# Linear attention: decays of the gates worked out ahead of the values' projection, two logarithms queued behind two exponentials

## The chip, the cores and the metric

The kernel runs on one core of one Trainium2 chip. The metric is device time in microseconds (us), the median of the runs shown. The engines are TensorE (PE, with its weight loads as PEld), VectorE (DVE), ScalarE (ACT), GpSimd (POOL) and SyncE (SP, which only issues transfers here).

## The reference

One layer of a generator. Two token mixers, a gated linear attention (GLA, 4 heads) and a gated delta rule (GDN, 8 heads), read the same normed input of 1024 latent and 256 context tokens; their outputs are gated, merged and projected, a feed-forward network follows, and a norm. The change is within GLA:

```python
def gla_prepare(q, k, v, lr_f, lr_b, lr_w, lr_bias):        # heads of 128 (q, k) and 256 (v)
    gates = tuple(log_sigmoid(lr @ lr_w[d] + lr_bias[d]) / 16 for d, lr in ((0, lr_f), (1, lr_b)))

def step(S, inp):                                            # gla_scan, chunk by chunk, in both directions
    qc, kc, vc, gc = inp
    G = cumsum(gc, axis=-2)
    decay = exp(where(incl[:, :, None], G[..., :, None, :] - G[..., None, :, :], -inf))
    A = einsum('bhid,bhjd,bhijd->bhij', qc, kc, decay)
    o = einsum('bhij,bhjv->bhiv', A, vc) + einsum('bhid,bhdv->bhiv', qc * exp(G), S)
    S = exp(G_end)[..., None] * S + einsum('bhjd,bhjv->bhdv', kc * exp(G_end - G), vc)
```

## The kernel before, in words

Three phases follow one another. **Phase 1** (to about 797 us) holds the input norm and, for each of the four GLA heads in turn, `gla_head`, and then six projections with convolution for GDN (`gdn_conv`, six behind each head by `CONVS`). **Phase 2** is the GDN scan with the merges, **phase 3** the output projection and the feed-forward network.

Products with large weights run as three matmuls of split operands (`mm3`, L174 to L176). The weights come by `wcols`: `wsplit` loads a tile on SP's queue (`wraw`, tag "wr", 2 buffers) and splits it into `whi` on ACT (L156) and `wlo` on DVE (L157), tags "wh" and "wl", 4 buffers each. The values of a head need four such tiles, other projections of a head two.

A head works in this order: queries (L443), keys (L450), values (`v`, five pairs of chunks through the three banks "pj", copied out on DVE at L458), in head 0 the low-rank input of the gates and its loads (`gla_lowrank`), then the **decays**. Of these, L471 makes the gates' logits (three matmuls for each direction, banks "ch", of which there are three), L472 and L474 take the absolute value and the minimum with zero, L477 the exponential, L479 the logarithm, L483 and L490 sum along the chunks, L498 takes the decay of a chunk. `decayed_keys` (L502 to L520) multiplies the keys by a decay (`e`, L514), transposes them on PE (L517) and copies them out (`kt`, L519); L528 and L538 multiply them with `v` into the states `S` (L529, L539). The attention over seven levels follows (L544 to L610), then the six convolutions: projection, copies out of the banks on ACT (L788 to L792), taps on DVE (L797, L800), a tanh (L802) and a product (L803). `mod_rows`, called behind the keys, adds up a row of the modulation on DVE (L1092).

Each engine works off its own list in order. The lists are laid out at compile time by a planner that takes, of what its own clock holds to be ready, what stands earliest in the program; `high_priority` moves an instruction forward, and `issue_after` ties the instructions of a block on one engine behind a given one. So work that stands later, such as a convolution's projection, fills in where a head waits. `q`, `k`, `v`, `G` and `S` have one buffer each: a head can write them only when the head before has read them for the last time.

Of the kernel before, what the change touches and what calls it, by code (L numbers as in the profile page):

```python
# [8 lines left out]
F32 = mybir.dt.float32  # L9
# [3 lines left out]
AF = mybir.ActivationFunctionType  # L13
# [4 lines left out]
P = 128  # L18
D = 1024
KT = D // P  # L20
# [3 lines left out]
NCH = TT // P  # L24
# [7 lines left out]
C_GQ, C_GK, C_GV, C_GZ, C_LR, _, C_DQ, C_DK, C_DV, C_DZ, C_AB, C_G1, C_G2 = (int(o) for o in OFF[:13])  # L32
# [46 lines left out]
class Layer:  # L79
# [354 lines left out]
    def gla_head(self, h):  # L434
        nc, I, g1, g2 = self.nc, self.I, self.g1, self.g2
# [3 lines left out]
        w = self.wcols(I['w_in'], C_GQ + h * P) if h else self.first  # L439
        for t0, n in spans[:2]:  # L440
            ps = self.pj(P, 512)
# [4 lines left out]
        w = self.wcols(I['w_in'], C_GK + h * P)  # L446
        for t0, n in spans:
            ps = self.pj(P, 512)[:, 0:n]
            self.proj(ps, w, t0, n)
            nc.scalar.activation(k[:, t0:t0 + n], ps, AF.Copy)  # L450
        yield 1
        v = g1.tile([P, NCH, 256], F32, name="v")
        w = self.wcols(I['w_in'], C_GV + h * 256, 256)
        for c0 in range(0, NCH, 2):
            ps = self.pj(P, 2, 256)
            for c in (c0, c0 + 1):
                self.mm3(ps[:, c - c0, :], [self.xparts(kk, c * P, P) + w[kk] for kk in range(KT)])
            nc.vector.tensor_copy(v[:, c0:c0 + 2, :], ps)  # L458
        yield 2
        if h == 0:  # L460
            self.gla_lowrank()

# [3 lines left out]
        ts = [s.rearrange("p c n -> p (c n)")[:, 0:TT] for s in S]  # L466
        zs = []
        for d, t in enumerate(ts):
            for t0, n in spans:
                ps = self.ch(P, 512)[:, 0:n]  # L470
# [3 lines left out]
                    nc.vector.tensor_scalar(G[:, 0, t0:t0 + n], ps, 0.0, None, ALU.min)  # L474
                zs.append(ps)
        for t in ts:
            nc.scalar.activation(t, t, AF.Exp, scale=-1.0)  # L477
        for t in ts:
            nc.scalar.activation(t, t, AF.Ln, bias=1.0)  # L479
        chunks = [(c * P, P) for c in range(8)] + [(T, TC)]  # L480
        for c0, n in chunks:
            g = G[:, 0, c0:c0 + n]
# [14 lines left out]
        for d in range(2):  # L497
            nc.scalar.activation(dec[d], end[d], AF.Exp, scale=1.0 / 16)  # L498

        def decayed_keys(d, c0, nch):  # L500

            lo, n = c0 * P, nch * P  # L502
            e = g2.tile([P, 4, P], F32, tag="e", name="e", bufs=4)
            ef = e.rearrange("p c i -> p (c i)")[:, 0:n]
            if d == 1:
                nc.scalar.activation(ef, G[:, 1, lo:lo + n], AF.Exp, scale=1.0 / 16)
            else:
                if lo < T:
                    nc.vector.tensor_tensor(e[:, 0:nch], end[0][:, c0:c0 + nch].unsqueeze(2).broadcast_to([P, nch, P]),
                                            Gf[:, c0:c0 + nch], ALU.subtract)  # L510
                else:
                    nc.vector.tensor_scalar(ef, G[:, 0, lo:lo + n], G[:, 0, TT - 1:TT], -1.0, ALU.subtract, ALU.mult)
                nc.scalar.activation(ef, ef, AF.Exp, scale=1.0 / 16)
            nc.vector.tensor_tensor(ef, ef, k[:, lo:lo + n], ALU.mult)  # L514
            ps = self.wk(P, 4, P)
            for c in range(nch):
                nc.tensor.transpose(ps[:, c, :], e[:, c, :], self.ident)  # L517
            kt = g2.tile([P, 4, P], F32, tag="kt", name="kt", bufs=2)
            nc.scalar.activation(kt[:, 0:nch], ps[:, 0:nch], AF.Copy)  # L519
            return kt  # L520


        for d in range(2):
            first = 0 if d == 0 else 7
            kt = decayed_keys(d, 8, 2)
            ps = self.ch(P, 512)[:, 0:256]
            for c in range(2):
                nc.tensor.matmul(ps, kt[:, c, :], v[:, 8 + c, :], start=(c == 0), stop=(c == 1))  # L528
            nc.scalar.activation(S[d][:, first, :], ps, AF.Copy)  # L529
            self.dump(f"gla_s{h}_{d}", S[d][:, first, :])  # L530
            for half in ((0, 1) if d == 0 else (1, 0)):
                cs = (range(0, 4), range(4, 7)) if d == 0 else (range(1, 4), range(4, 8))
                cs = cs[half]
                kt = decayed_keys(d, cs[0], len(cs))
                for c in (cs if d == 0 else reversed(cs)):
                    nxt = c + 1 if d == 0 else c - 1
                    ps = self.ch(P, 512)[:, 0:256]
                    nc.tensor.matmul(ps, kt[:, c - cs[0], :], v[:, c, :], start=True, stop=True)  # L538
                    nc.vector.scalar_tensor_tensor(S[d][:, nxt, :], S[d][:, c, :], dec[d][:, c:c + 1], ps, ALU.mult, ALU.add)  # L539
# [4 lines left out]
        for half in range(2):  # L544
            c0, lo = 4 * half, 512 * half
# [5 lines left out]
            ps = self.wk(P, 4, P)  # L551
# [4 lines left out]
            for li, s in enumerate(LEVELS):  # L556
# [19 lines left out]
                ps = self.wk(P, 4, P)  # L576
# [12 lines left out]
            for c in range(c0, c0 + 4):  # L589
                cs = slice((c - c0) * P, (c - c0) * P + P)  # L590
                ps = self.ch(P, 512)[:, 0:256]
# [12 lines left out]
            for j in range(2):  # L604
                ps = self.wk(P, 4, P)
# [823 lines left out]
```

## Time and profile before

| | |
|---|---|
| runs | 2364.49, 2360.04, 2384.71 us; median 2364.49 |
| the profiled execution | 2363.35 us, its span 2361.6 us |
| busy share of the span | PE 96%, PEld 80%, DVE 73%, ACT 49%, POOL 4% |
| mean granted TensorE clock | 0.985 of full speed |

The profiled execution spends 1.75 us outside its span. A busy share is a mean over stages: DVE with 73% is nearly full in some stretches of phase 1 and nearly empty in others. The granted clock has two levels, 1.2 and 2.4 GHz, shown as 0.50 and 1.00.

### The profile page before, as it was taken

What the parts mean: (1) busy time and instruction counts of PE and PEld (TensorE: products, weight loads), DVE (VectorE), ACT (ScalarE), POOL (GpSimd) and SP (SyncE); (2) the same over time, 40 slices, a digit from 0 to 9 for tenths busy, and PEclk for the clock granted to TensorE, in tenths of its full rate; (3) what the DMA queues carried; (4) which work ended last, traced back from release to release, by engine and by line L of the source; (5) the groups of instructions that cost most, each with busy time, mean ns of one, the idle gap of its engine ahead of it and who ended that gap; (6) DMA issues with size and microseconds to landing.
All of it is one profiled execution on the core that took longest, in us unless ns stands there. A gap on an engine that the chain in (4) does not pass through costs nothing. (4 is left out here: it accounts for less than half of the span.)

```text
span 2361.6 us, 37155 instructions
## 1 busy us (share of the span) xinstructions
PE 2273.9 (96%) x13604; PEld 1885.6 (80%) x13604; DVE 1713.0 (73%) x4087; ACT 1167.6 (49%) x2803; POOL 96.7 (4%) x190
## 2 busy tenths in 40 slices
PE   7999999999999899999999999989999999999998
PEld 4988888888888777877787787768778888888886
DVE  6579669669669675988888788565687777783454
ACT  6265355355355556678678776643433333341221
POOL 0000000000000100000000000000000000000000
PEclk9999999999999999999999998999999999999999
DMA  8212402401501542323323332233132222264221
GB/s 287 68 38 72 148 18 64 161 19 60 165 18 59 171 116 81 114 74 100 109 81 96 101 110 71 90 133 131 54 112 94 85 76 90 77 205 138 88 77 58
DMA packets 208166, 230.82 MB, mean 98 GB/s; under 512 B 14835, under 2 KB 170811, under 8 KB 207983
## 3 DMA queue, kind: packets, MB, share of 16 engines
q1 hardware_dynamic: 189040, 171.18, 24.5%
q0 software_dynamic: 14688, 50.92, 5.9%
q10 hardware_dynamic: 4255, 6.35, 0.9%
q8 instruction: 107, 1.75, 0.3%
q14 instruction: 76, 0.62, 0.1%
HBM read 181.44 MB, written 46.96 MB: 97 GB/s over the span
## 5 line engine op out<-in xcount | busy, mean ns | idle before, releaser
L174 PE MATMUL pj<-xh,whi 128*128 128x512 f32 x1304 | 530.3, 407 | 4.7 <-ACT cout L789 3.2
L176 PE MATMUL pj<-xh,wlo 128*128 128x512 f32 x1304 | 528.8, 407 | 5.1 <-DVE wlo L157 2.8
L175 PE MATMUL pj<-xl,whi 128*128 128x512 f32 x1304 | 529.3, 406 | 0.9 <-DVE xl L1167 0.6
L176 PEld LDWEIGHTS pj<-xh,wlo 128*128 128x128 f32 x1304 | 248.3, 190 | 49.1 <-DVE wlo L157 3.1
L174 PEld LDWEIGHTS pj<-xh,whi 128*128 128x128 f32 x1304 | 248.6, 191 | 48.8 <-ACT cout L789 3.8
L175 PEld LDWEIGHTS pj<-xl,whi 128*128 128x128 f32 x1304 | 248.4, 190 | 43.8 <-DVE xl L1167 1.2
L156 ACT ACTIVATE whi<-wraw 128x512 fp32r<-128x512 f32 x144 | 90.1, 629 | 147.0 <-PE pj L176 84.1
L157 DVE TENSOR_TENSOR wlo<-wraw,whi 128x512 fp32r<-128x512 f32 x144 | 97.7, 686 | 25.9 <-ACT whi L156 25.7
L797 DVE SCALAR_TENSOR_TENSOR cout<-cin,cw,cout 128x896 f32<-128x896 f32 (+1 forms) x96 | 113.1, 1178 | 4.1 <-ACT cout L789 4.1
L1246 ACT ACTIVATE whi<-s 128x512 fp32r<-128x512 f32 x88 | 54.8, 629 | 118.0 <-DVE s L1253 43.0
L1374 ACT ACTIVATE ahi<-araw 128x512 fp32r<-128x512 f32 (+1 forms) x48 | 28.5, 594 | 158.2 <-PE pj L175 131.0
L1375 DVE TENSOR_TENSOR alo<-araw,ahi 128x512 fp32r<-128x512 f32 (+1 forms) x48 | 30.8, 643 | 80.7 <-ACT ahi L1374 80.7
L1246 ACT ACTIVATE whi<-wraw 128x512 fp32r<-128x512 f32 x60 | 37.9, 632 | 102.7 <-PE pj L175 49.4
L967 DVE TENSOR_TENSOR X<-X,D 128x30 f32<-128x30 f32 (+14 forms) x240 | 78.3, 326 | 2.0
L965 DVE TENSOR_TENSOR D<-X 128x30 f32<-128x30 f32 (+14 forms) x240 | 78.1, 325 | 2.1
L1280 DVE TENSOR_TENSOR B<-pj,B 128x512 f32<-128x512 f32 x79 | 54.2, 686 | 28.6 <-PE pj L176 28.6
L174 PE MATMUL pj<-whi,xh 128*128 128x256 f32 x256 | 73.4, 287 | 0.0
L175 PE MATMUL pj<-wlo,xh 128*128 128x256 f32 x256 | 72.4, 283 | 0.0
L176 PE MATMUL pj<-whi,xl 128*128 128x256 f32 x256 | 72.4, 283 | 0.0
L458 DVE COPY v<-pj 128x512 f32<-128x512 f32 x20 | 13.8, 691 | 79.6 <-PE pj L176 79.4
L174 PE MATMUL ch<-q,whi 128*128 128x512 f32 x176 | 68.6, 390 | 1.0 <-ACT whi L1246 1.0
L176 PE MATMUL ch<-q,wlo 128*128 128x512 f32 x176 | 68.5, 389 | 0.0
(464 smaller groups left out, 5848.3 us busy)
## 6 DMA issues: line engine op xcount, KB each, us to landing
wraw<-in_w_in_dram SPq DMA_DIRECT2D x144, 256.0 KB, 3.0
mw<-in_w_mod_dram SPq DMA_DIRECT2D x64, 256.0 KB, 3.3
wraw<-in_ffn_w_gate_dram SPq DMA_DIRECT2D x22, 512.0 KB, 3.7
wraw<-in_ffn_w_up_dram SPq DMA_DIRECT2D x22, 512.0 KB
draw<-in_ffn_w_down_dram SPq DMA_DIRECT2D x22, 512.0 KB, 4.8
acts<-B POOLq DMA_DIRECT2D x42, 256.0 KB, 2.3
bc<-rows SPq DMA_DIRECT2D x80, 128.0 KB, 3.2
araw<-acts SPq DMA_DIRECT2D x40, 256.0 KB, 2.9
```

What stands on the lines that cost most here:

```text
L156: nc.scalar.activation(hi, raw, AF.Copy)
L157: nc.vector.tensor_tensor(lo, raw, hi.bitcast(F32), ALU.subtract)
L174: self.nc.tensor.matmul(ps, ah, bh, start=(first and i == 0), stop=False)
L175: self.nc.tensor.matmul(ps, ah, bl, start=False, stop=False)
L176: self.nc.tensor.matmul(ps, al, bh, start=False, stop=(last and i == n - 1))
L797: nc.vector.scalar_tensor_tensor(o, cl[:, :, lo + s:16 + hi + s], tap(i), o, ALU.mult, ALU.add)
L965: nc.vector.tensor_tensor(tmp, X[:, j:j + 1, j + 1:32].broadcast_to([P, j, n]), X[:, 0:j, j:j + 1].broadcast_to([P, j, n]), ALU.mult)
L967: nc.vector.tensor_tensor(X[:, 0:j, j + 1:32], X[:, 0:j, j + 1:32], tmp, ALU.add)
L1246: nc.scalar.activation(hi, src, AF.Copy)
L1280: add = lambda o, a, b: nc.vector.tensor_tensor(o, a, b, ALU.add)
L1374: nc.scalar.activation(hi, raw, AF.Copy)
L1375: nc.vector.tensor_tensor(lo, raw, hi.bitcast(F32), ALU.subtract)
```

## The change

The block that projects the values moves from behind the keys to behind the decays, with its loads, its copies and the generator's third stop. With it, `gla_lowrank` of head 0 and all instructions of the decays up to L498 now stand in the program ahead of it; `decayed_keys` and what follows stand behind it, as before. And both logarithms are tied, on ACT, behind the second exponential.

```diff
         yield 1
-        v = g1.tile([P, NCH, 256], F32, name="v")
-        w = self.wcols(I['w_in'], C_GV + h * 256, 256)
-        for c0 in range(0, NCH, 2):
-            ps = self.pj(P, 2, 256)
-            for c in (c0, c0 + 1):
-                self.mm3(ps[:, c - c0, :], [self.xparts(kk, c * P, P) + w[kk] for kk in range(KT)])
-            nc.vector.tensor_copy(v[:, c0:c0 + 2, :], ps)
-        yield 2
         if h == 0:
             self.gla_lowrank()
...
         for t in ts:
-            nc.scalar.activation(t, t, AF.Exp, scale=-1.0)
-        for t in ts:
-            nc.scalar.activation(t, t, AF.Ln, bias=1.0)
+            exp = nc.scalar.activation(t, t, AF.Exp, scale=-1.0)
+        with self.tc.issue_after(exp.ins):
+            for t in ts:
+                nc.scalar.activation(t, t, AF.Ln, bias=1.0)
...
         for d in range(2):
             nc.scalar.activation(dec[d], end[d], AF.Exp, scale=1.0 / 16)
 
+        v = g1.tile([P, NCH, 256], F32, name="v")
+        w = self.wcols(I['w_in'], C_GV + h * 256, 256)
+        for c0 in range(0, NCH, 2):
+            ps = self.pj(P, 2, 256)
+            for c in (c0, c0 + 1):
+                self.mm3(ps[:, c - c0, :], [self.xparts(kk, c * P, P) + w[kk] for kk in range(KT)])
+            nc.vector.tensor_copy(v[:, c0:c0 + 2, :], ps)
+        yield 2
         def decayed_keys(d, c0, nch):
```

## Rows read from the trace of the kernel before

**Rows 1.** The page's first line: busy time of each engine, with its share of the span.

```profile
PE 2273.9 (96%) x13604; PEld 1885.6 (80%) x13604; DVE 1713.0 (73%) x4087; ACT 1167.6 (49%) x2803; POOL 96.7 (4%) x190
```

**Rows 2.** The first line of the waits of PE, which are sorted by their total: who waited <- for whom: us in total, times, longest.

```profile
PE wk L517 <- DVE e L514: 10.9, 4, 3.2
```

**Rows 3.** Stretches of 20 us. Columns: stretch, us, then busy us (instructions) of PE, PEld, DVE, ACT, POOL, granted clock, DMA share, GB/s.

```profile
140.00:160.00 20.00, 16.84 (x88) 13.84 (x87) 17.27 (x41) 15.99 (x31) 0.00 (x0) 0.91 0.06 14
...
180.00:200.00 20.00, 20.00 (x98) 16.78 (x97) 19.96 (x37) 9.11 (x22) 0.60 (x1) 1.00 0.24 72
200.00:220.00 20.00, 18.59 (x112) 15.90 (x111) 18.38 (x39) 12.68 (x21) 1.63 (x3) 1.00 0.25 87
...
320.00:340.00 20.00, 16.79 (x92) 14.10 (x91) 17.23 (x41) 14.40 (x30) 0.00 (x0) 0.91 0.06 14
...
500.00:520.00 20.00, 16.77 (x88) 13.86 (x87) 17.85 (x43) 12.73 (x28) 0.00 (x0) 0.91 0.06 14
...
660.00:680.00 20.00, 18.19 (x104) 15.61 (x102) 12.13 (x29) 17.11 (x23) 0.00 (x0) 1.00 0.10 27
680.00:700.00 20.00, 18.60 (x95) 15.52 (x96) 18.04 (x43) 10.92 (x25) 0.00 (x0) 0.91 0.06 14
...
780.00:800.00 20.00, 15.85 (x61) 11.98 (x60) 14.03 (x25) 9.49 (x17) 3.23 (x6) 0.84 0.47 148
```

**Rows 4.** Stretches of 1 us in head 3, the same columns.

```profile
681.00:682.00 1.00, 0.60 (x3) 0.60 (x4) 1.00 (x4) 0.81 (x3) 0.00 (x0) 0.53 0.00 0
682.00:683.00 1.00, 1.00 (x6) 1.00 (x6) 1.00 (x3) 0.87 (x3) 0.00 (x0) 0.50 0.03 8
683.00:684.00 1.00, 1.00 (x3) 0.75 (x3) 0.99 (x4) 0.74 (x2) 0.00 (x0) 0.50 0.00 0
684.00:685.00 1.00, 1.00 (x7) 0.79 (x6) 1.00 (x3) 0.34 (x2) 0.00 (x0) 0.76 0.00 0
```

**Rows 5.** PE in order of time, head 0, from the gates' logits to the first state: start, us, instruction, count, and in brackets the idle time before and what ended it.

```profile
129.24 0.63 PE L471 MATMUL ch<-lr,lw 128*128 128x512 f32 x2
...
144.28 0.28 PE L176 MATMUL pj<-xch,wlo 128*128 128x256 f32 x1
146.48 0.50 PE L174 MATMUL pj<-xh,whi 128*128 128x512 f32 x1 [1.92 <-ACT cout L789]
148.22 0.44 PE L517 MATMUL wk<-cf,e 128*128 128x128 f32 x2 [1.24 <-DVE e L514]
...
151.44 1.74 PE L538 MATMUL ch<-v,kt 128*128 128x256 f32 x6
```

**Rows 6.** ACT in order of time over the same stretch.

```profile
133.40 1.34 ACT L472 ACTIVATE S<-ch 128x512 f32<-128x512 f32 x3
...
136.05 1.27 ACT L479 ACTIVATE S<-S 128x1280 f32<-128x1280 f32 x1
137.34 1.28 ACT L477 ACT_TABLE_LOAD   x1
...
144.75 0.58 ACT L788 ACTIVATE cin<-pj 128x512 f32<-128x512 f32 x1
```

**Rows 7.** The loads of a table at the logarithms' line: duration in ns (least/median/most), first and last start.

```profile
L479 ACT ACT_TABLE_LOAD  x8: 1283/1283/1283, 134.8 to 673.6; - x8
```

**Rows 8.** DVE in order of time over the stretch of rows 5.

```profile
137.35 3.22 DVE L483 TENSOR_TENSOR_SCAN G<-G,S 128x128 f32<-128x128 f32 x9 [4.71 <-ACT S L479]
143.04 1.62 DVE L486 SCALAR_TENSOR_TENSOR S<-ch,S 128x512 f32<-128x512 f32 x3 [1.03 <-ACT S L479]
...
147.74 1.03 DVE L514 TENSOR_TENSOR e<-e,k 128x256 f32<-128x256 f32 x2
```

**Rows 9.** DVE in order of time while the values of head 0 are projected: two of the five copies of `v`.

```profile
98.39 0.69 DVE L458 COPY v<-pj 128x512 f32<-128x512 f32 x1 [5.07 <-PE pj L176]
104.15 0.69 DVE L458 COPY v<-pj 128x512 f32<-128x512 f32 x1 [5.07 <-PE pj L176]
```

**Rows 10.** The end of the values' projection in head 1, all engines in order of time.

```profile
306.05 1.35 ACT L156 ACTIVATE whi<-wraw 128x512 fp32r<-128x512 f32 x2 [27.58 <-PE pj L176]
...
308.01 0.75 PE L471 MATMUL ch<-lr,lw 128*128 128x512 f32 x3
...
308.59 0.39 PE L174 MATMUL pj<-xh,whi 128*128 128x512 f32 x1
```

**Rows 11.** ACT in order of time in head 0: the first split of `gla_lowrank`.

```profile
113.51 0.63 ACT L408 ACTIVATE lhi<-lraw 128x512 fp32r<-128x512 f32 x1 [26.31 <-PE pj L176]
```

**Rows 12.** A line of the waits of ACT over the whole span: splits that waited for their transfer.

```profile
ACT whi L156 <- DMA wraw<-in_w_in_dram: 32.0, 25, 3.1
```

**Rows 13.** DVE's groups of the convolutions from 148 to 252 us (head 0's states and attention): line, operation, shape, count | busy us, mean ns | idle before.

```profile
L797 DVE SCALAR_TENSOR_TENSOR cout<-cin,cw,cout 128x896 f32<-128x896 f32 x10 | 11.5, 1147 | 1.6 <-ACT cout L789 1.6
...
L803 DVE SCALAR_TENSOR_TENSOR cout<-cin,cout 128x1280 f32<-128x1280 f32 x4 | 5.9, 1486 | 0.0
...
L800 DVE SCALAR_TENSOR_TENSOR cout<-cin,cw,cout 128x255 f32<-128x255 f32 x8 | 3.8, 480 | 0.0
```

**Rows 14.** PE in order of time where phase 1 passes into phase 2.

```profile
787.34 0.50 PE L174 MATMUL pj<-xh,whi 128*128 128x512 f32 x1 [1.26 <-ACT cout L789]
...
794.42 0.39 PE L720 MATMUL wk<-par,sel 8*80 8x4 f32 x2 [2.89 <-DMA wraw<-in_w_in_dram]
```

**Rows 15.** PE in order of time: eight transposes in the attention of head 0.

```profile
204.68 1.25 PE L607 MATMUL wk<-cf,o 128*128 128x128 f32 x8 [1.41 <-DVE o L602]
```

## The prediction

> **What bounds the kernel now.** The page comes first: PE is busy for 96% of the span [rows 1], and the other engines matter only where they make PE wait. So the next view is the waits of PE. Their first line is the place that the change touches: the transposes of the decayed keys (L517) wait for the product `e` (L514), 10.9 us in four waits, one for each head [rows 2]. Then the stretches of 20 us. PE is full nearly everywhere in phase 1, and the exceptions repeat once for each head: 16.84, 16.79 and 16.77 us of 20 in heads 0 to 2, and in head 3 18.19 and 18.60 in two neighbouring stretches [rows 3]. In the same places the granted clock is 0.91 instead of 1.00. The stretches of 1 us show why: behind the idle time PE works at 0.50, the lower of the two levels (1.2 GHz), through the four stretches shown, and is then back at the upper one [rows 4].
>
> The order of time explains the gap. In head 0 the logits of the gates start at 129.24, the first transpose at 148.22, so the chain of the decays takes 19.0 us. Beneath it PE finds a convolution's projection, which ends at 144.28 + 0.28; then there is a lone matmul, since the banks wait for copies on ACT, and two idle pieces of 1.92 and 1.24 us [rows 5]. The copies (L788) come only at 144.75 because exponentials, logarithms and table loads stand ahead of them [rows 6].
>
> **What the change removes.** *The idle time.* Taken from the stretches it is 3.16 + 3.21 + 3.23 + (1.81 + 1.40 = 3.21) = 12.8 us over four heads [rows 3]. It is more than the 10.9 us of [rows 2] because the wait for ACT's copies belongs to the same gap. With the change the projection of the values stands behind the decays. Two copies of it are 5.76 us apart [rows 9], so five pairs of chunks give 28.8 us of PE work above a chain of 19.0 us. That work does not need the decays, nor the decays it. The chain even gets shorter (see ACT and DVE below). So I count the 12.8 us as gone, with a cover that is 28.8 - 19.0 = 9.8 us too long; to lose it the chain would have to grow by half.
>
> *The low clock.* In head 3 the loss of clock is 0.47 + 0.50 + 0.50 + 0.24 = 1.7 us of PE at the upper level [rows 4]; in heads 0 to 2, a mean of 0.91 over 20 us gives 1.8 each [rows 3]. I take 4 x 1.7 = 6.8 us. In each head the fall comes behind the idle time, and PE is counted as full while it is low, so if the idle time goes I expect the fall to go with it.
>
> **What it moves on ACT and DVE.** The order exponential, load, logarithm, load, exponential, load, logarithm becomes two exponentials, one load, two logarithms. Per head one of the two loads at the logarithms (1.28 us each, two for each head [rows 7]) and the one at the second exponential [rows 6] go: 4 x 2 x 1.28 = 10.3 us of ACT. None of it is on the path that sets the end once the values cover the chain, so it adds nothing to the sum. The tie adds a wait: the first logarithm stands behind the second exponential. Before, it ended at 136.05 + 1.27 = 137.32. After, with the absolute values ending at 133.40 + 1.34 = 134.74 [rows 6], it ends at 134.74 + 1.27 + 1.28 + 1.27 = 138.6, some 1.2 us later, and the second at 139.8, where DVE got it at 143.04 before [rows 8]. Behind the waiting logarithm on ACT stands only what needs it. On DVE the first scans (L483), which sat idle for 4.71 us [rows 8], wait 1.2 us longer, and copies of `v` (L458) can be queued behind them. Of the three banks two more pairs can be projected meanwhile, 2 x 5.76 = 11.5 us, so PE does not see it. From 139.8 the second direction's subtraction, scans and the product take what they took from 143.04 to 147.74 + 1.03: 5.7 us. The chain then ends at 145.5 on this clock, 16 us after its start.
>
> **What it moves on PE and the queues.** The 13 to 14 us of a convolution that filled the gap (129.24 to 144.56, less the logits) move into the states and the attention behind. PE was full there too, so nothing is won or lost by that; DVE, at 19.96 of 20 us [rows 3], gets that work later. Three costs no row shows:
>
> - *The join behind the values.* Now the transposes follow at once, and the chain transpose, copy, state is late next. Upper bound: from L517 to the first L538 took 151.44 - 148.22 = 3.2 us [rows 5], for each head 12.9 us in all, if no convolution stands ready. Lower bound: nothing, since at the same join before, the next weights were split from 306.05, ahead of the end, and a projection ran at 308.59 behind the logits at 308.01 [rows 10], without a gap. That row is the nearer; I take 0.5 us a head, 2 us.
> - *Head 0's low-rank input* goes ahead of the values, with its loads on ACT's queue (L381, L403), SP's (L431) and its stores on POOL's (L426); the four loads of the values' weights go behind them on SP. Before, its first split sat idle for 26.31 us because buffers were held by the values' weights [rows 11]; now only queries and keys stand ahead. Bounds: nothing, or one load that comes too late, at most 3.1 us [rows 12]. I take 1 us, nearer to the first, as the keys' projection lies above it.
> - *The passage into phase 2.* The attention of head 3 ends earlier, its last convolutions later. The waits there are 1.26 and 2.89 us [rows 14], the clock 0.84 over 20 us, another 3.2 us [rows 3]. All of that, 7.4 us, could go, or 4.2 us of idle time could come again. I take nothing.
>
> **The sum**, against the profiled execution: 2363.35 - 12.8 - 6.8 + 2 + 1 = 2346.7 us. The median of the runs shown is 1.1 us above that execution, so I say 2347. The kernels of such a comparison can be told apart by about 1%, here 2340.9 and 2388.1 us: what I forecast is real, yet lies within it.
>
> **A rule against it.** Eight transposes in head 0's attention, at 204.68 [rows 15], lie in a stretch with a granted clock of 1.00 although PE idled 1.41 us there [rows 3]. The Trainium skill, "TensorE: Matmul & The Clock Gate" (Part 4: PE-mode transpose), says that the full clock does not engage for transposes, as they don't count as busy work. By that rule the transposes themselves, not the idle time, would pull the clock down; the trace speaks against it.
>
> **The rivals.**
>
> 1. *The clock falls anyway* at the transposes of L517, whatever stands ahead. For it: in each head the low clock begins with them. Against it: [rows 3, 15]. It keeps 6.8 us: 2353.5. Chance 0.05.
> 2. *A new wait at the join or in head 0*, near the upper bounds above. The gain falls by 6 to 10 us: 2353 to 2357. For it: the values hold all four weight buffers, so a convolution's weights can be split only as the last chunk is projected. Against it: [rows 10]. Chance 0.16.
> 3. *The passage gains*: its 7.4 us go too, 2339. For it: the buffers of the attention come free earlier. Against it: one of the waits is for a transfer. Chance 0.12.
> 4. *Nothing changes*: the gap only moves, for instance because another engine sets the pace of a head, and the time stays at 2364. Chance 0.07.
> 5. *Slower, by DVE's backlog in the attention.* A convolution costs DVE 4 x 1.15 + 4 x 0.48 + 1.49 = 8.0 us [rows 13]. It is projected later than before, when DVE is full, and the next head's queries can't be written until the attention has read the old ones. If one such piece ends late in each head, PE waits 4 x 8.0 = 32 us, against 19.6 won: 2376. It decides from 4.9 us of backlog a head. Against it: during the values DVE sits idle for 5.07 of each 5.76 us [rows 9], and the 13 us of decays that it did with PE waiting are done there now. Chance 0.05.
>
> **How the numbers follow.** My forecast keeps 0.55, as the cover is known from rows and only the small joins are not. The range reaches from rival 3, with a little room (2337), to the upper end of rival 2 (2359); it leaves out rivals 4 and 5 and a tail. Faster by over 1%: rival 3 and a sliver of the forecast, 0.13. Slower by over 1%: the far end of rival 5, 0.02. Within 1%: 0.85.
>
> **What will show it.** If I am right, the line L517 <- L514 is gone from PE's waits or below 1 us in all; the stretches around the states show PE full at a clock of 1.00 in all four heads; the loads of a table at the logarithms are 4 instead of 8; each head, from one start of the logits to the next, is some 5 us shorter. PE's total of busy time falls a little, by the matmuls no longer done at the low level. I am wrong if L517 or L528 wait for the copy `kt`, if the clock falls at the transposes without idle time, if head 0 shows PE waiting for the low-rank weights, or if the gap comes back at the end of the attention or in phase 2, whose order the planner lays out anew.

## The result, and the profile after

Measured beside each other, the kernel before had a median of 2374.24 us and the changed one 2336.28 us; the ratio is 0.9878 with an interval of 0.9832 to 0.9924. On the 2364.49 us shown ahead of the prediction that is 2335.6 us (2324.8 to 2346.5). The forecast was 2347.0, its range 2337 to 2359: the sign was right and the gain too small, 17.5 us against some 29. The measured median lies 0.7 us below the lower end of the range, the 2335.6 us 1.4 below it, and both on the other side of the bound of 1% than the forecast; a gain of over 1% had a chance of 0.13.

In some executions TensorE works through some 50 us of phase 2 at the lower level of its clock and the time is then some 20 us longer (2355.81 us of the four of after and, by their times, 2384.71 and 2384.0 of the four of before), so that without them the medians are 2362.3 and 2336.1 us, 26.2 us apart. On the 2364.49 us that gives 2338.3, inside the range. The profiled execution of after (span 2354.0) is one of these, so its phase 1 is read here, and the rest from a second measurement of the same kernel (2336.77 us, span 2335.0, called "after again" below).

The page's first line:

```profile
PE 2277.9 (97%) x13604; PEld 1890.4 (80%) x13604; DVE 1718.8 (73%) x4087; ACT 1157.4 (49%) x2795; POOL 96.9 (4%) x190
```

PE's waits from the logits of head 0 to phase 2 (95 to 766 us), a single line:

```profile
PE pj L174 <- ACT cout L790: 1.3, 1, 1.3
```

Against [rows 1], ACT issues 8 instructions fewer and is busy 10.2 us less. The wait of the transposes for `e` [rows 2] is gone; of the two waits at the passage [rows 14], the one for a convolution's copy stays and the one of 2.89 us is gone.

The stretches of 20 us that hold the transposes in heads 0 to 3, one with the transposes of [rows 15] in head 0's attention (now at 178.40), and two at the passage (columns as in [rows 3]):

```profile
120.00:140.00 20.00, 19.96 (x141) 17.97 (x140) 14.00 (x29) 9.08 (x19) 0.00 (x0) 1.00 0.16 41
...
160.00:180.00 20.00, 20.00 (x108) 17.22 (x107) 16.05 (x36) 9.65 (x24) 0.60 (x1) 1.00 0.19 60
...
300.00:320.00 20.00, 19.96 (x116) 16.83 (x115) 17.39 (x38) 9.77 (x19) 0.00 (x0) 1.00 0.16 40
...
460.00:480.00 20.00, 19.96 (x151) 18.55 (x151) 13.56 (x29) 8.63 (x18) 0.00 (x0) 1.00 0.15 37
640.00:660.00 20.00, 19.96 (x128) 17.46 (x127) 14.71 (x31) 8.50 (x17) 0.00 (x0) 1.00 0.17 40
...
760.00:780.00 20.00, 18.73 (x90) 14.79 (x90) 14.84 (x36) 11.83 (x25) 2.98 (x6) 1.00 0.64 206
780.00:800.00 20.00, 16.32 (x76) 12.49 (x75) 9.13 (x31) 13.67 (x61) 1.27 (x3) 1.00 0.65 205
```

Where [rows 3] had a clock of 0.91 and 16.8 us of PE in heads 0 to 2 (in head 3 the idle time lay across two stretches), there are now 1.00 and 19.96 us in each head. At the passage the clock is 1.00 where it was 0.84. The join in head 0, on PE in order of time:

```profile
100.43 0.63 PE L463 MATMUL ch<-lr,lw 128*128 128x512 f32 x2
...
130.47 0.28 PE L176 MATMUL pj<-whi,xcl 128*128 128x256 f32 x1
130.59 1.29 PE L518 MATMUL wk<-cf,e 128*128 128x128 f32 x8
131.72 1.03 PE L529 MATMUL ch<-v,kt 128*128 128x256 f32 x4
132.58 1.96 PE L539 MATMUL ch<-v,kt 128*128 128x256 f32 x8
```

No line has an idle time in brackets, unlike [rows 5]: values, transposes, first state follow one another. The chain of the decays beneath it on ACT, in order of time:

```profile
103.36 1.27 ACT L469 ACTIVATE S<-S 128x1280 f32<-128x1280 f32 x1
...
105.91 1.27 ACT L469 ACTIVATE S<-S 128x1280 f32<-128x1280 f32 x1
107.20 1.28 ACT L472 ACT_TABLE_LOAD   x1
108.49 2.43 ACT L472 ACTIVATE S<-S 128x1280 f32<-128x1280 f32 x2
```

On DVE:

```profile
109.80 3.22 DVE L476 TENSOR_TENSOR_SCAN G<-G,S 128x128 f32<-128x128 f32 x9 [1.35 <-ACT S L472]
...
117.60 0.68 DVE L499 COPY v<-pj 128x512 f32<-128x512 f32 x1
...
119.07 0.42 DVE L515 TENSOR_TENSOR e<-e,k 128x256 f32<-128x256 f32 x1
```

And the line of the logarithms, its table loads over the whole kernel:

```profile
L472 ACT ACT_TABLE_LOAD  x4: 1283/1283/1283, 107.2 to 621.3; - x4
```

The first `e` is ready at 119.07 + 0.42 = 119.49, 19.1 us after the logits, and its transpose comes at 130.59: 11.1 us to spare. The loads are 4 instead of 8 [rows 7].

**Where the time went.** The logits of heads 0 to 3 start at 100.43, 272.25, 443.94 and 615.23 us, 171.8, 171.7 and 171.3 apart, where before it was 129.24, 308.01, 485.69 and 663.57, 178.8, 177.7 and 177.9 apart: 7.0, 6.0 and 6.6 us for each head. The first matmul of phase 2 comes at 765.81 instead of 794.42, 28.6 us earlier:

```profile
765.81 0.30 PE L721 MATMUL wk<-par,sel 8*80 8x4 f32 x2
```

Taken from one end of the keys' copies to the next, the same place in both programs, the first three heads gain 6.5, 6.0 and 6.2 us, and from the last keys to phase 2 (150.9 us instead of 160.5) it is 9.5; 0.4 us lie ahead of the first keys. From that matmul to the end of the span, after again needs 1569.4 us and before 1567.2, so 2.2 us are given back in phases 2 and 3, where PE idles 55.9 us instead of 52.5. From span to span the gain is 26.6 us (2361.6 to 2335.0). The 28.6 us up to phase 2 split like this:

| what | forecast | after |
|---|---|---|
| idle time at the transposes, four heads | -12.8 | -12.8 |
| low clock behind it | -6.8 | -6.8 |
| the join behind the values | +2 | 0 |
| head 0's low-rank input | +1 | 0 |
| wait in head 0's attention, 1.41 us before | 0 | -1.4 |
| wait at the passage, 2.89 us before | 0 | -2.9 |
| the rest | 0 | -4.7 |
| up to phase 2 | -16.6 | -28.6 |

The rest is what is left when idle time and clock are taken off. Some 0.7 us of it are order alone: three matmuls of one product stand ahead of the first matmul of phase 2 in before and behind it in after. Otherwise PE's matmuls stand a little closer together, start to start, at the upper clock. In head 1 that is about 1.1 us; the cause was not looked for further and stays open.

### The profile page after: what moved, and what is told of

The parts are those of the page before. It is cut to its first block, busy times and chain, and to the rows that moved or that the text cites. A ratio compares the mean times of both kernels' runs of the same rounds, so it can differ in the third digit from the quotient of the medians.

```text
span 2354.0 us, 37175 instructions
## 1 busy us (share of the span) xinstructions
PE 2277.9 (97%) x13604; PEld 1890.4 (80%) x13604; DVE 1718.8 (73%) x4087; ACT 1157.4 (49%) x2795; POOL 96.9 (4%) x190
## 5 line engine op out<-in xcount | busy, mean ns | idle before, releaser
L994 PEld LDWEIGHTS wk<-Y,M 32*32 32x32 f32 (+1 forms) x960 | 50.0, 124 | 27.3 <-issue 7.5
```

What stands on the lines that cost most here:

```text
L994: nc.tensor.matmul(p1[lo, u, :], M[hi, u, lo], Y[hi, u, 64 - size:64], start=True, stop=True)
```

## The experiments

**The kernel as it is, once more, and the move without the tie.** Is it the cover or the tie that brings the gain?

> The changed kernel once more. The 51.2 us of lower clock in phase 2 of its first profile stand in one execution of four and should not be here. If nothing that phase 1 won is given back, the first matmul of phase 2 (L721) starts near 766 us and the span ends some 1568 us later, at 2334; the kernel before needs 1567 from there. If phase 2 gives back, that second part is 1573 or more. Against the kernel before: 24 to 28 us less.

```diff
             exp = nc.scalar.activation(t, t, AF.Exp, scale=-1.0)
-        with self.tc.issue_after(exp.ins):
-            for t in ts:
-                nc.scalar.activation(t, t, AF.Ln, bias=1.0)
+        for t in ts:
+            nc.scalar.activation(t, t, AF.Ln, bias=1.0)
```

> Only the values' block is moved; the logarithms are not tied, so there are again two loads of a table at their line for each head. If the cover does it (theory 1), the time is within 3 us of the changed kernel, no wait at L517's place, clock 1.00 in phase 1. If the shorter chain on ACT does a part of it (theory 2), gaps of 1 us or more for each head come back at the transposes and the gain is 5 to 15 us smaller.

After again: ratio 0.9922, interval 0.9873 to 0.9971. The move alone: 0.9883, 0.9843 to 0.9922. Most of the distance between the two is the long low stretch in phase 2, by the granted clock (0.979 to 0.982 instead of 0.989 to 0.994) three of six executions against one of six; without them the medians are 2335.5 and 2333.5 us. In the move alone, phase 2 starts at 765.9 us against 765.6, PE idles 1.8 us from the keys of head 0 to there against 1.6. All of PE's waits from 95 to 766 us:

```profile
PE pj L174 <- ACT cout L789: 1.3, 1, 1.3
PE ch L538 <- ACT kt L519: 0.2, 1, 0.2
```

The line of the logarithms has as many table loads as before [rows 7]:

```profile
L471 ACT ACT_TABLE_LOAD  x8: 1283/1283/1283, 105.6 to 625.8; - x8
```

So the gain is the move's, all of it as far as these runs can tell; the loads that the tie saves lie beneath the values and are worth nothing, as the prediction had counted them.

**The tie without the move.** The kernel after, with the values' block back in its old place:

```diff
         yield 1
+        v = g1.tile([P, NCH, 256], F32, name="v")
+        w = self.wcols(I['w_in'], C_GV + h * 256, 256)
...
+        yield 2
         if h == 0:
             self.gla_lowrank()
...
             exp = nc.scalar.activation(t, t, AF.Exp, scale=-1.0)
         with self.tc.issue_after(exp.ins):
```

> Only the tie: the values stay ahead of the decays, both logarithms queue behind both exponentials. The chain on ACT is 2 loads (2.6 us) shorter. Theory 1 (the cover does it): the gap of 3.2 us a head shrinks to 0.5 to 2 us but stays; where it no longer makes the clock fall, 1.7 us a head go with it; gain 3 to 12 us. Theory 2 (the chain does it): the gap goes, gain 18 us or more.

It is slower than before: 2381.79 us, ratio 1.0097 (1.0067 to 1.0127). I had not expected that by any theory. PE's first two waits of phase 1 (95 to 816 us):

```profile
PE wk L579 <- DVE ek L574: 16.8, 12, 2.1
PE wk L518 <- DVE e L515: 9.1, 4, 2.5
```

A stretch of 20 us in head 1's attention:

```profile
340.00:360.00 20.00, 13.75 (x74) 12.30 (x73) 17.33 (x38) 6.23 (x10) 0.00 (x0) 0.75 0.00 0
```

The gap at the transposes shrinks only from 10.9 [rows 2] to 9.1 us, and 16.8 us of new waits appear in the attention, with a low clock behind them: at the levels (L579) PE has nothing else to do, it waits 1.4 us on average (16.8 in 12), and phase 2 starts 20.8 us later. In the changed kernel not one of these waits exists.

**Where that loss sits: the tie in head 3 alone, then with earlier weight splits, and a control.** The first edit, against the tie without the move:

```diff
-        with self.tc.issue_after(exp.ins):
+        with ExitStack() as tie:
+            if h == 3:
+                tie.enter_context(self.tc.issue_after(exp.ins))
```

> The kernel before with the tie of the logarithms in head 3 alone, the values where they were. With the tie in all heads and the values in place the kernel had become slower, its phase 2 starting 20.8 us later, although the gap at the transposes shrank to 2 to 2.5 us a head. Theory 1 (the tie itself is harmless or a small gain; the loss came from the lists that the planner lays out anew in heads that have a next head): phase 2 starts within 2 us of 794.4, the gap at head 3's transposes is 2 to 3 us, the time within 0.2 percent of before. Theory 2 (the tie costs in each head, by the later first logarithm or by what it queues behind itself on ScalarE): about 5 us, a quarter of the 20.8, phase 2 at 799 to 800, the time 0.2 to 0.3 percent above before.

Phase 2 starts at 797.9 us, and the last head takes 137.2 us from its logits to it, against 794.42 - 663.57 = 130.9 before: 6.3 more, though the gap at its transposes is 2.0 instead of 3.2 us. The ratio is 1.0054 (1.0027 to 1.0081). So the loss of one head is near the 5 us of theory 2, though phase 2 starts a little earlier than it said and the ratio is above its 0.2 to 0.3 percent; the size of the gap is as by theory 1. Stretches of 5 us (columns as in [rows 3]):

```profile
697.00:702.00 5.00, 4.61 (x36) 4.21 (x34) 4.88 (x12) 2.19 (x4) 0.00 (x0) 1.00 0.00 0
702.00:707.00 5.00, 1.22 (x9) 1.09 (x9) 5.00 (x11) 1.53 (x3) 0.00 (x0) 0.89 0.00 0
707.00:712.00 5.00, 2.92 (x12) 2.65 (x13) 4.11 (x10) 1.58 (x3) 0.00 (x0) 0.50 0.00 0
```

Two levels on PE there, and the split of weights that follows on DVE, in order of time:

```profile
703.70 1.13 PE L581 MATMUL wk<-eq,ek 128*128 128x128 f32 x8 [2.08 <-DVE ek L576]
706.91 2.05 PE L581 MATMUL wk<-eq,ek 128*128 128x128 f32 x8 [2.08 <-DVE ek L576]
...
711.48 0.68 DVE L157 TENSOR_TENSOR wlo<-wraw,whi 128x512 fp32r<-128x512 f32 x1
```

DVE is full here (5.00 of 5 us) with the levels' products, at 3.2 us for one level, and PE has nothing beside them: the second half of the next convolution's weights is split only at 711.48, behind the products of these levels. In the kernel before the same split stood at 702.07 and PE was full. Theory 2's mechanism, that the later logarithm or what stands behind it on ACT costs the time, does not show in these rows: nothing on PE waits for either, and ACT is idle for most of the stretch. The next two runs, one execution each, pull the splits of the six convolutions behind head 3 forward (400 in place of 100), with and without the tie; the first lines stand in `gdn_conv`, the last in `wsplit`.

```diff
+        self.soon = 400 if h >= 6 else SOONER
         w = self.wcols(self.I['w_in'], (C_DQ, C_DK, C_DV)[kind] + h * P)
+        self.soon = SOONER
...
-        with self.tc.high_priority(offset=SOONER):
+        with self.tc.high_priority(offset=self.soon):
```

> The kernel with the tie in head 3 alone, and one edit more: the splits of the weights of the last six convolutions (those behind head 3, which fill in beneath its decays and its attention) get a stronger pull forward in the planner, 400 in place of 100. In the kernel with the tie alone, the second half of a convolution's weights stood ready (its first split by 675 us) but was split on VectorE only at 711.48; TensorE had no projection to fill the attention and idled 2.08 us three times for ek, then ran at 0.50: the last head took 137.2 us from its logits to phase 2 instead of 130.9. Theory A (the late split is what costs, the tie itself does not): the split comes before 700, the waits for ek in head 3 are gone, and the last head takes 127 to 131 us. Theory B (the tie costs by what it holds up on ScalarE): the last head stays at 135 to 139 us.

> The control: the kernel before, without any tie, with the same stronger pull for those six convolutions' splits. In the kernel before, TensorE is full through head 3's attention, so an earlier split has nothing to win there. Theory A and B both: the gap of 3.2 us at head 3's transposes stays, the last head takes 130 to 131.5 us from its logits to phase 2. If it becomes shorter by some us here too, the pull has a gain of its own, which must then be taken off from what the other kernel shows.

With the tie, two stretches of 5 us in the first block of levels and two in the second:

```profile
700.00:705.00 5.00, 5.00 (x27) 4.13 (x26) 4.84 (x11) 1.85 (x4) 0.00 (x0) 1.00 0.22 52
705.00:710.00 5.00, 5.00 (x42) 4.92 (x42) 5.00 (x12) 4.13 (x7) 0.00 (x0) 1.00 0.00 0
...
750.00:755.00 5.00, 2.08 (x9) 1.78 (x8) 4.11 (x10) 1.96 (x4) 0.00 (x0) 0.68 0.00 0
755.00:760.00 5.00, 2.27 (x9) 2.03 (x10) 4.04 (x8) 0.63 (x1) 0.00 (x0) 0.50 0.00 0
```

The largest of PE's waits from 660 to 800 us:

```profile
PE wk L583 <- DVE ek L578: 5.2, 3, 2.1
```

The split now comes at 698.72, and the hole at 702 to 712 is closed: that hole did hang on the late split. But the same hole opens in the second block of levels at 750 to 760, where the next splits come at 756.70 and 759.55, and the last head takes 138.5 us. Theory A is right for the first hole, but the waits for `ek` are not gone, and the last head's time is the one that theory B gave (135 to 139 us). Its reason, that the tie holds something up on ACT, does not show: in both holes PE waits for DVE and DVE only for PE (1.9 us from 695 to 715, 2.1 us from 745 to 765), neither for ACT. The control has 129.8 us for its last head and no such wait, so the pull itself costs nothing. What is shown: in both runs with the tie and the values in their old place, a block of levels in head 3 is left without a projection beside it, not the same block in both. Why the splits come so late there stays open.

**Each head by itself.** Move and tie in one head alone, the other three as before; `values()` is the moved block, and the second run has 3 in place of 0:

```diff
+        moved = h in (0,)
+        if not moved:
+            v = values()
...
+        if moved:
+            v = values()
```

> Move and tie in head 0 alone; heads 1 to 3 as in the kernel before. From head 0's keys on, its values stand behind the low-rank input of the gates. Theory 1 (each head wins on its own, head 0 as much as the others, so its low-rank input costs nothing): the logits of head 1 start 6 to 8 us after those of head 0 less than before, 171 to 172 us instead of 178.8, the other two periods stay at 177 to 178, phase 2 starts 6 to 8 us earlier than 794.4, and the time is 2353 to 2358 against a before of 2360 to 2364. Theory 2 (head 0 pays for the low-rank input that now stands ahead of the values, as I had counted with 1 us and a bound of 3.1): the gain is 3 to 5 us and PE shows waits for a transfer or for the split of weights between 86 and 100 us. Note that in head 0 the logits themselves start 29 us earlier where the move is made, so the period to head 1, whose logits stand behind its values as before, is to be taken to the same place in the program: from the keys of head 0 to the logits of head 1.

> Block moved and logarithms tied in head 3 alone. If each head wins on its own (idle 3.2, clock 1.7, about 1 us of finer order) and the passage into phase 2 wins 3 us by the last head alone, 9 us less than before. If the passage needs the gain of all heads, 6 us. The gaps of heads 0 to 2 stay at 3.2 us each with a clock of 0.50 behind them.

Head 0 alone: the logits of head 1 start at 301.32 instead of 308.01, 6.7 us earlier, the other periods are 178.0 and 177.8, phase 2 starts 7.8 us earlier, ratio 0.9968 (0.9937 to 0.9999). No wait stands between the keys and the logits of head 0, so its low-rank input costs nothing: theory 1. Head 3 alone: ratio 0.9957 (0.9941 to 0.9973), phase 2 12.5 us earlier. Of this 9.4 us are the last head's (151.1 us from its keys to phase 2 against 160.5), 1.5 us an earlier start of head 0 in that execution, and the rest a slightly other order of the earlier heads. The waits for `e`, whole kernel, of head 0 alone:

```profile
PE wk L527 <- DVE e L524: 9.7, 3, 3.2
```

Of head 3 alone:

```profile
PE wk L527 <- DVE e L524: 7.7, 3, 3.2
```

Three waits are left in each, one for each head that was not moved. So head 0 wins by itself, 6 to 7 us, and the last one about 9, because behind it the wait of 2.89 us at the passage goes too. With heads 1 and 2, not tried alone, taken as head 0, that adds up to what the whole change shows.

**How long is the cover?** Extra work on ACT between the second exponential and the logarithms, in all heads, six copies and in the second run fourteen; they take 1.3 us each.

```diff
         with self.tc.issue_after(exp.ins):
+            for _ in range(6):
+                nc.scalar.activation(ts[0], ts[0], AF.Copy)
             for t in ts:
```

> The changed kernel with six extra copies of a 128x1280 tile onto itself on ScalarE, between the second exponential and the logarithms, in every head. The result stays the same. In the changed kernel an exponential of that size took 1.27 us, so the chain of the decays grows by about 6 x 1.27 = 7.6 us a head. In head 1 of the changed kernel the first product e is ready at 289.97 us, and the transposes that need it come at about 302, so 10 to 12 us are spare. Theory 1 (the values' projection is a cover with that much to spare, nothing else was late): no wait at the transposes, phase 2 starts within 2 us of the changed kernel's 765.6, the time of an undisturbed run is 2332 to 2340. Theory 2 (the cover is already used up, because copies of v on VectorE or the copies of the convolutions on ScalarE stand behind the chain): a gap comes back in each head and with it the low clock, 4 to 7.6 us plus 1.7 a head, phase 2 starts at 788 to 803 and the time is 2355 to 2372.

> The same with fourteen copies, about 17.8 us more of chain in each head, which is more than the 10 to 12 us to spare. Theory 1 (cover of fixed length): a gap of 17.8 less 10 to 12, so 6 to 8 us a head, and behind it a low clock that costs about 1.7: 30 to 39 us more than the changed kernel, so 2362 to 2375, phase 2 starting at 796 to 805. Theory 2 (later work, such as a convolution's projection, fills in once the values are through, as it did in the kernel before): the gap stays below 3.3 us a head, at most 5 with the clock, and the time is 2340 to 2356. If chain_plus6 costs nothing and this one costs much, the spare cover lies between 7.6 and 17.8 us.

Six copies: phase 2 starts at 767.76, 2.2 us later than in after again, the ratio to before is 0.9912 (0.9877 to 0.9947), with the long low stretch in five of ten executions and a median of 2336.9 us in the other five; the logits stay 172.9, 172.3 and 171.4 us apart. PE's two longest waits of phase 1 are these, and the only new one above 0.5 us is 1.1 us in two heads, for a copy of `v`:

```profile
PE pj L174 <- ACT cout L792: 1.3, 1, 1.3
PE ch L531 <- DVE v L501: 1.1, 2, 0.8
```

Fourteen copies: 2382.79 us, ratio 1.0104 (1.0066 to 1.0142), slower than the kernel before, with phase 2 at 813.27; theory 1 had said 2362 to 2375 us and 796 to 805. PE's largest waits of phase 1:

```profile
PE pj L174 <- DVE v L501: 10.5, 4, 3.6
PE wk L581 <- DVE ek L576: 6.2, 3, 2.1
```

Stretches of 5 us in head 1:

```profile
320.00:325.00 5.00, 2.25 (x13) 1.51 (x11) 3.87 (x11) 4.27 (x6) 0.00 (x0) 1.00 0.00 0
325.00:330.00 5.00, 3.29 (x9) 2.41 (x10) 4.88 (x10) 2.66 (x6) 0.00 (x0) 0.56 0.00 0
330.00:335.00 5.00, 4.31 (x13) 3.16 (x12) 2.91 (x7) 1.91 (x4) 0.00 (x0) 0.50 0.21 54
```

DVE there:

```profile
321.13 3.21 DVE L478 TENSOR_TENSOR_SCAN G<-G,S 128x128 f32<-128x128 f32 x9 [5.12 <-ACT S L474]
...
325.71 0.68 DVE L501 COPY v<-pj 128x512 f32<-128x512 f32 x1
```

The gap is back: 2.75 + 1.71 + 0.69 = 5.2 us of idle time in head 1. The chain grew by some 18 us there (fourteen copies of 1.29), so some 13 us of that were covered, near the 12.0 us to spare in head 1 of the changed kernel (first `e` ready at 290.28, transposes at 302.29). Theory 1 in its mechanism, with two things beyond it. One I had mis-sized: the low clock behind this gap costs 2.2 + 2.5 us in the last two stretches shown and 0.45 in the next, 5.1 us instead of 1.7. Idle time and clock make 10.3 us, and the period to the next logits is 182.2 instead of 171.7, 10.5 more. The other I had not expected: in head 0 the period is 190.4 instead of 171.8, since the three waits for `ek` at the levels, 6.2 us, all lie there. The rows also say what PE waits for: not the transposes' `e`, but a copy of `v`, which is queued on DVE behind the scans that wait for the logarithm, so that a bank comes free late and the last pair of the values can't be projected. The prediction named that queue, and took two more pairs in the free banks, 11.5 us, as enough.

## Why the prediction came out as it did

- *The gap goes.* Right in size: 12.8 us of idle time in four heads, now 0.04 us in each stretch. The move alone and the head-by-head runs show that the cause is the place of the values.
- *The low clock goes with it.* Right: 1.00 through the transposes and the states in all four heads. Rival 1 falls: the transposes at 130.59 run within a stretch of clock 1.00, and fourteen copies bring gap and low clock back together. The Trainium skill ("TensorE: Matmul & The Clock Gate", Part 4: PE-mode transpose) says that the full clock does not engage for transposes; the trace does not agree, with 1.00 in that stretch.
- *Cover and chain.* The cover was right, 130.59 - 100.43 = 30.2 us from logits to transposes against the 28.8 forecast. The chain was not: I had it shrink from 19.0 to 16 us, and it takes 19.1 us in head 0. I let the second direction's subtraction on DVE start as soon as its logarithm is there, 10.6 us after the logits, though by my own figures the first direction's scans hold DVE until 138.6 + 3.2 = 141.8, 12.6 us after them; in the trace it starts at 112.93, 12.5 us after. A copy of `v` (117.60) ahead of the first `e` adds 0.6. The two errors leave a spare of 11 us where I had said 9.8 without and some 13 with the shorter chain.
- *ACT's loads on no path.* Right, by the move without the tie.
- *The join, +2 us, and the low-rank input, +1 us.* Both too careful, both measured at 0. I took a value between bounds; the row that I had called the nearer [rows 10] gave no cost at the join, and it was right.
- *The passage, 0.* Mis-sized by 2.9 us up to phase 2: the wait for the transfer went, the one for the copy stayed. Rival 3 was this mechanism with 7.4 us, and at the place 6.1 of them came, for the 3.2 us of low clock are gone too (1.00 from 780 to 800). But phases 2 and 3 take 2.2 us longer in spite of it, so that some 0.7 us of the passage is left in the time: on balance the 0 was near, by luck.
- *Not in the sum:* 1.4 us of a wait in head 0's attention that [rows 3, 15] showed and that I put down to no cause, and the 4.7 us of the rest, which I read in no view of the kernel before.
- *Rivals 2, 4 and 5* did not happen. The holes that PE had in the attention with the tie alone and with fourteen copies show that rival 5's place, the levels beside a busy DVE, is where such a change can lose. The move avoids it here; whether because more projections are left for the attention was not tried.

The large terms, 19.6 us, came as forecast. Each small term was set on the careful side, 3 us of costs that were nothing and 9 us of gains that were not counted; together they are the 12 us by which the gain up to phase 2 was too small. With the 2.2 us given back behind it, 9.8 us are left.

## What to carry to other kernels

A wait of a few us that returns at the same place of every pass is worth more than its length: add the low clock that may follow it (here 1.7 us behind 3.2 us of idle time, nothing behind 1.26 or 1.41), and the waits further on that it feeds. To hide a chain between engines, put behind its start a block that needs nothing of it, longer than the chain, and look for copies of that block which are queued behind the chain on another engine, for there the cover can end first. A tie that only saves work on an engine with time to spare brings nothing by itself, and where lists are laid out by a planner it can cost more than it saves.

## What the runs showed of the hardware

The long stretch of low clock in phase 2 was not expected. Stretches of 20 us of the profiled execution of after:

```profile
860.00:880.00 20.00, 17.21 (x101) 13.04 (x99) 11.11 (x26) 13.44 (x30) 0.96 (x2) 0.86 0.25 69
880.00:900.00 20.00, 20.00 (x140) 14.74 (x140) 3.59 (x9) 6.93 (x18) 1.43 (x3) 0.50 0.27 78
900.00:920.00 20.00, 20.00 (x151) 15.19 (x149) 4.61 (x14) 7.97 (x23) 0.85 (x2) 0.50 0.12 40
```

The first two of these in after again:

```profile
860.00:880.00 20.00, 16.69 (x106) 12.25 (x104) 7.53 (x16) 13.02 (x30) 0.47 (x2) 0.74 0.24 65
880.00:900.00 20.00, 20.00 (x252) 15.12 (x252) 7.87 (x21) 12.99 (x37) 2.23 (x5) 1.00 0.30 93
```

The same program at the same place has PE busy without a break, at 1.2 GHz in one execution, at 2.4 GHz in the other (140 against 252 matmuls in 20 us). In both the clock falls in the stretch before, in which PE is idle for 2.8 and 3.3 us; in one it is back at the upper level by 880, in the other PE stays at the lower level through 40 us of unbroken work. The profiled executions of the move alone and of the tie in head 3 have it too; of the kernel before only times some 20 us longer point to it. What decides it no run here shows.
